# Small constants loaded as rows and spread by one product, the fifth x block in another buffer, and a later last step of the bias table, in a two-layer hybrid trunk

## The chip, the cores and the metric

One core of a Trainium2 chip runs the whole program. The metric is the device time of one execution in microseconds (us), as the median of several runs. Differences are named against the time of the kernel before.

## What is computed

The reference is one inference step of a trunk of two layers, for 512 prompt tokens and 64 sample tokens (576 together) of width 1024, all in fp32. The part that matters here, cut from the reference:

```python
mod = silu(c) @ ada_w + ada_b                 # six pieces: shift, scale, gate, twice
h = rmsnorm(x, norm_mix_g) * (1 + sc_m) + sh_m
z, xbc, dt_raw, q, k, v, g_ssm, g_attn = split(h @ w_in)
dt = softplus(dt_raw + dt_bias);  a = -exp(a_log)      # per SSM head, 32 of them
y = ssd_scan(xs, dt, a, B, C) + xs * d_skip            # per SSM head
q = rmsnorm(q, q_norm_g);  k = rmsnorm(k, k_norm_g)    # 64 values each, per head
p = softmax(concat(q k^T / 8 + bias, sinks))           # sinks: per query head, 16 of them
```

The kernel keeps channels on the 128 partitions. So the constants by heads (`a_log`, `dt_bias`, `d_skip`, `sinks`) are needed repeated on every partition (the last two with even heads on partitions 0 to 63 and odd heads on 64 to 127), and the head norms (`q_norm_g`, `k_norm_g`) are needed as columns, twice one above the other. Then follow the two branches' projections, an output projection, and a gated feed-forward part; all large products go through the same helper.

## The kernel before, in words

**Products.** Each weight block of 1024 x 128 is a granule: SP loads it (L185), ScalarE rounds it to `whi` (L166), GpSimd or VectorE forms the rest `wlo` (L167), and TensorE makes three products for each of 8 blocks of rows and each half of the 576 tokens (L278 to L280): 48 products a projection. ScalarE or VectorE takes the sums out of PSUM.

**The order.** Python code emits instructions in the order of the text; a planner with a simulated timeline then fixes one order for each engine, and for SP's queue of DMAs, and may pull an instruction forward or push it back against the text where its inputs and buffers allow. On the chip each engine goes through its list strictly in order, so an instruction that waits holds all behind it. All DMAs of the kernel are issued on SP.

**The opening.** Five blocks of x (four of 128 tokens, one of 64, in `load_x`, L542) go through a four-buffer ring `w4` and are transposed; the fifth therefore needs a buffer back. The first modulation pieces are loaded in four quarters (L1581) and formed by `ada_quarter`. Three first projections (`leads`, L1615 to L1617) are summed quarter by quarter as the modulated, normalised x (`nt`, `hh`, `hl`) comes. Then a list of jobs runs: in layer 0 the projection for dt (job 0), four q projections, and x, z, B and C ones, with a modulation step (`Ada`, L324) after each from the third job on. Side work (the dt chain, convolution, scan, head norms, attention) is emitted between the pieces of jobs.

**Constants.** `const_loads` loads what lies in DRAM as rows of 128: modulation bias, two norms, scan norm, convolution bias (104 rows, tile `rows`), and convolution weights and state; `const_cols` and `const_rest` transpose them on TensorE (L491, L502, L503). `const_loads1` loads `d_skip`, `dt_bias` and `a_log` already spread over the partitions, `const_loads2` the head norms and the sinks; each tile is first touched by GpSimd (`hold`, L433), so that its load is not issued before some earlier result is there. The Exp of `a_log` stands in `const_rest` (helper line L159, tile `ea`), the negated sinks in `const_nsk` (L486). Layer 0's `const_loads1` is emitted after the last quarter's loads and its `const_loads2` after job 2; layer 1's come at job `C1` = 20 and its readers at job 28.

**The bias table.** `build_bias` is a generator of three steps, taken after the jobs `BI`, `BI+1` and `BI+3` with `BI` = 3: the relative bias is transposed, unrolled into a vector and stored in DRAM (L595); strips of it are loaded back, shifted row by row (L604, tile `rt`); a product with a flipped identity puts them in place (L610, `bflip`), VectorE copies them (L613) and SP stores them (L614). Attention loads the table from there.

Of the kernel before, what the change touches and what calls it, by code (L numbers as in the profile page):

```python
# [12 lines left out]
ALU = mybir.AluOpType  # L13
# [38 lines left out]
def hybrid_trunk(ctx: ExitStack, tc: tile.TileContext, I, O):  # L52
# [376 lines left out]
    after = []  # L429

    def hold(l, t):

        G.tensor_copy(out=t[:, 0:1], in_=L[0]["mod"][:, 2, 0, 0:1] if l else after[0])  # L433

    def const_loads(l):
        c = L[l]
        rowsA = w2("rows", [128, 3, 128])
        rows = c["rows"] = rowsA[:, 2]
        if l:
            hold(l, rows)  # L440
        off = 0
        for src, n in ((I["ada_b"][l], 48), (I["norm_mix_g"][l], 8), (I["norm_ffn_g"][l], 8),
                       (I["ssm_norm_g"][l], 16), (I["conv_b"][l], 24)):
            SY.dma_start(out=rows[off:off + n, :], in_=src.rearrange("(t c) -> t c", c=128))
            off += n
        rowsB = c["rowsB"] = rowsA[:, 0:2]
        if l:
            hold(l, rowsB[:, 0])
            hold(l, rowsB[:, 1])
        SY.dma_start(out=rowsB[0:96, 0, :], in_=I["conv_w"][l].rearrange("k (t c) -> (k t) c", c=128))  # L450
        SY.dma_start(out=rowsB[0:72, 1, :], in_=I["state_conv"][l, 0].rearrange("k (t c) -> (k t) c", c=128))

    def const_loads1(l):
        c = L[l]
        dsk = c["dsk"] = con.tile([128, 16], F32, name=f"dsk{l}")
        hold(l, dsk)
        dv = I["d_skip"][l].rearrange("(m r) -> r m", r=2)
        for r in range(2):
            SY.dma_start(out=dsk[64 * r:64 * r + 64, :], in_=dv[r].partition_broadcast(64))
        dtb = c["dtb"] = con.tile([128, 32], F32, name=f"dtb{l}")  # L460
        hold(l, dtb)
        SY.dma_start(out=dtb, in_=I["dt_bias"][l].partition_broadcast(128))
        ea = c["ea"] = con.tile([128, 32], F32, name=f"ea{l}")
        hold(l, ea)
        SY.dma_start(out=ea, in_=I["a_log"][l].partition_broadcast(128))

    def const_loads2(l):
        c = L[l]
        qkg = con.tile([128, 2], F32, name=f"qkg{l}")
        hold(l, qkg[:, 0:1])  # L470
        hold(l, qkg[:, 1:2])
        for j, nm in enumerate(("q_norm_g", "k_norm_g")):
            for r in range(2):
                SY.dma_start(out=qkg[64 * r:64 * r + 64, j:j + 1], in_=I[nm][l].rearrange("(p o) -> p o", o=1))
        c["qg"], c["kg"] = qkg[:, 0:1], qkg[:, 1:2]
        snk = con.tile([128, 8], F32, name=f"snk{l}")
        hold(l, snk)
        sv = I["sinks"][l].rearrange("(c h) -> h c", h=2)
        for r in range(2):
            SY.dma_start(out=snk[64 * r:64 * r + 64, :], in_=sv[r].partition_broadcast(64))  # L480
        c["snk"] = snk

    def const_nsk(l):
        c = L[l]
        nsk = c["nsk"] = con.tile([128, 8], F32, name=f"nsk{l}")
        V.tensor_scalar(out=nsk, in0=c["snk"], scalar1=-1.0, scalar2=None, op0=ALU.mult)  # L486

    def const_cols(l):
        c = L[l]
        ps = sps("cT")  # L490
        T.transpose(ps[:, 0:104], c["rows"][0:104, :], ident[0:104, 0:104])  # L491
        colA = con.tile([128, 104], F32, name=f"colA{l}")
        V.tensor_copy(out=colA, in_=ps[:, 0:104])
        V.tensor_scalar(out=colA[:, 64:104], in0=colA[:, 64:104], scalar1=0.5, scalar2=None, op0=ALU.mult)
        c["colA"] = colA
        c["ssmg"], c["convb"] = colA[:, 64:80], colA[:, 80:104]
        c["mod"] = con.tile([128, 6, 8, 2], F32, name=f"mod{l}")

    def const_rest(l):
        c = L[l]  # L500
        ps = sps("cB")
        T.transpose(ps[:, 0:96], c["rowsB"][0:96, 0, :], ident[0:96, 0:96])  # L502
        T.transpose(ps[:, 96:168], c["rowsB"][0:72, 1, :], ident[0:72, 0:72])  # L503
        colB = con.tile([128, 4, 24], F32, name=f"colB{l}")
        S.mul(out=colB.rearrange("p k t -> p (k t)"), in_=ps[:, 0:96], mul=0.5)
        stc = con.tile([128, 3, 24], F32, name=f"stc{l}")
        V.tensor_copy(out=stc.rearrange("p k t -> p (k t)"), in_=ps[:, 96:168])
        act(c["ea"], c["ea"], ACTF.Exp)
        c["convw"], c["stc"] = colB, stc
        c["ncv"] = con.tile([128, 2, 3, 24], F32, name=f"ncv{l}")  # L510
# [22 lines left out]
    def load_x(xb):  # L533
# [4 lines left out]
        for i in range(5):  # L538
            n = 128 if i < 4 else 64
            src = I["x_prompt"][0, i * 128:(i + 1) * 128, :] if i < 4 else I["x_sample"][0]  # L540
            xn = w4("xn", [128, 1024])
# [1049 lines left out]
    after.append(raws[3][1][:, 7, 255:256])  # L1591
    const_loads1(0)
# [5 lines left out]
    const_rest(0)  # L1598
    xhs = [next(xgen)]
# [30 lines left out]
    for i, j in enumerate(jobs):  # L1630
# [11 lines left out]
        if i == 2:  # L1642
            after[0] = f32(nm0.hh[1][:, 3, TOK - 1:TOK])
            const_loads2(0)
        if i in (BI, BI + 1, BI + 3):
# [3 lines left out]
        if i == C1:  # L1649
            const_loads(1)  # L1650
            const_loads1(1)
            const_loads2(1)
        if i == C1 + 8:
            const_cols(1)
            const_rest(1)
            for l in range(DEPTH):
                const_nsk(l)
# [39 lines left out]
```

## Time and profile before

| | |
|---|---|
| median of 3 runs | 2643.12 us (2639.3 to 2647.48) |
| the profiled execution | 2642.57 us |
| its span, first to last instruction | 2640.7 us, 49241 instructions |
| mean granted TensorE clock | 0.986 |
| TensorE busy | 2527.7 us (96%), 19605 matmuls |
| VectorE busy | 1605.9 us (61%) |
| ScalarE, GpSimd busy | 1059.0 us, 1054.5 us (40% each) |
| moved by DMA | 294.40 MB, 111 GB/s on average |

Of the span's forty slices of 66 us, the page gives TensorE's busy tenths as 6, 8, 9, 6 for the first four and 9 or more for all others; the granted clock is 8, 9, 9, 7 tenths in those four and 9 in the rest. PE is TensorE, DVE VectorE, ACT ScalarE, POOL GpSimd, and SPq SP's queue of DMAs. An arrow in square brackets gives the idle time before an instruction and what ended it.

### The profile page before, as it was taken

Reading aid. Unit: us, or ns where it says so; the run is one execution under the profiler, and the core shown is the slowest. Engines: PE = TensorE matmul, PEld = TensorE weight load, DVE = VectorE, ACT = ScalarE, POOL = GpSimd, SP = SyncE. Lnnn points to the kernel's source line nnn. Section 1 sums busy time; section 2 is a strip of 40 time slices with the busy share of each in tenths; the row PEclk is TensorE's granted clock in tenths of the full one; section 3 lists DMA queues with packets and bytes.
Section 4 is the critical chain, followed back from the end, with each engine's and each line's share of the span. In section 5 each row is a group of like instructions: output and inputs, shape, how many; then the busy total and the mean of one; then the engine's idle time right before and its main releaser. Section 6 shows DMA issues by size and latency. Waiting matters only on the chain. (4 is left out here: it accounts for less than half of the span.)

```text
span 2640.7 us, 49241 instructions
## 1 busy us (share of the span) xinstructions
PE 2527.7 (96%) x19605; PEld 2399.6 (91%) x19605; DVE 1605.9 (61%) x2981; ACT 1059.0 (40%) x2383; POOL 1054.5 (40%) x980
## 2 busy tenths in 40 slices
PE   6896999999999999999989999999999999999999
PEld 5785898999889999999989899989998899999999
DVE  4376949564765665655576997767456656444443
ACT  3343544433444542222245554544434445323222
POOL 3343544434223774544476544544432257000000
PEclk8997999999999999999999999999999999999999
DMA  7444542333212554544465333232421245322322
GB/s 207 122 154 127 149 114 86 95 83 98 57 49 83 159 166 139 153 152 151 155 175 145 93 111 102 85 95 84 104 72 50 60 128 155 96 87 81 88 77 72
DMA packets 471556, 294.40 MB, mean 111 GB/s; under 512 B 76544, under 2 KB 453856, under 8 KB 471328
## 3 DMA queue, kind: packets, MB, share of 16 engines
q1 hardware_dynamic: 471328, 291.27, 38.4%
q8 instruction: 154, 2.52, 0.4%
q14 instruction: 74, 0.61, 0.1%
HBM read 277.07 MB, written 13.16 MB: 110 GB/s over the span
## 5 line engine op out<-in xcount | busy, mean ns | idle before, releaser
L167 POOL TENSOR_TENSOR wlo<-raw,whi 128x512 fp32r<-128x512 f32 (+1 forms) x632 | 901.4, 1434 | 895.8 <-ACT whi L166 841.2
L278 PE MATMUL dps<-hh,whi 128*128 128x288 f32 x3536 | 1058.8, 300 | 18.6 <-DVE gate L153 13.9
L279 PE MATMUL dps<-hh,wlo 128*128 128x288 f32 x3536 | 1049.6, 297 | 2.8 <-POOL wlo L167 2.8
L280 PE MATMUL dps<-hl,whi 128*128 128x288 f32 x3536 | 1050.2, 297 | 1.1 <-DVE hl L156 1.1
L278 PEld LDWEIGHTS dps<-hh,whi 128*128 128x128 f32 x3536 | 667.0, 189 | 42.8 <-issue 21.5
L166 ACT CAST whi<-raw 128x512 fp32r<-128x512 f32 (+1 forms) x762 | 462.5, 610 | 576.4 <-PE dps L280 424.4
L279 PEld LDWEIGHTS dps<-hh,wlo 128*128 128x128 f32 x3536 | 667.8, 189 | 8.7 <-POOL wlo L167 4.9
L280 PEld LDWEIGHTS dps<-hl,whi 128*128 128x128 f32 x3536 | 667.4, 189 | 6.1 <-issue 4.4
L279 PE MATMUL dps<-ah,wlo 128*128 128x288 f32 x704 | 209.9, 298 | 3.1 <-POOL wlo L167 3.1
L278 PE MATMUL dps<-ah,whi 128*128 128x288 f32 x704 | 207.8, 295 | 4.6 <-DVE x L153 2.4
L280 PE MATMUL dps<-al,whi 128*128 128x288 f32 x704 | 207.7, 295 | 0.0
L153 DVE SCALAR_TENSOR_TENSOR ada_acc<-araw,csl,ada_acc 128x1024 f32<-128x1024 f32 x98 | 149.4, 1563 | 79.7 <-DMA araw<-in_ada_w_dram 73.4
L153 DVE SCALAR_TENSOR_TENSOR cv<-u,colB,cv 128x579 f32<-128x579 f32 x144 | 149.6, 1039 | 38.0 <-ACT cv L159 36.6
L278 PE MATMUL dps<-yh,whi 128*128 128x288 f32 x512 | 153.3, 299 | 9.1 <-ACT u L819 4.3
L280 PE MATMUL dps<-yl,whi 128*128 128x288 f32 x512 | 151.9, 297 | 0.0
L279 PE MATMUL dps<-yh,wlo 128*128 128x288 f32 x512 | 151.3, 296 | 0.0
L278 PEld LDWEIGHTS dps<-ah,whi 128*128 128x128 f32 x704 | 132.1, 188 | 6.1 <-issue 4.2
L279 PEld LDWEIGHTS dps<-ah,wlo 128*128 128x128 f32 x704 | 132.2, 188 | 5.6 <-POOL wlo L167 4.5
L167 DVE TENSOR_TENSOR wlo<-raw,whi 128x512 fp32r<-128x512 f32 (+1 forms) x124 | 83.7, 675 | 87.0 <-ACT whi L166 85.6
L280 PEld LDWEIGHTS dps<-al,whi 128*128 128x128 f32 x704 | 132.2, 188 | 0.2 <-DVE al L167 0.2
L278 PEld LDWEIGHTS dps<-yh,whi 128*128 128x128 f32 x512 | 96.2, 188 | 14.3 <-ACT u L819 5.8
L280 PEld LDWEIGHTS dps<-yl,whi 128*128 128x128 f32 x512 | 96.1, 188 | 1.5 <-issue 1.3
(331 smaller groups left out, 3869.4 us busy)
## 6 DMA issues: line engine op xcount, KB each, us to landing
raw<-in_w_in_dram SPq DMA_DIRECT2D x119, 512.0 KB, 4.0
raw<-in_w_gate_up_dram SPq DMA_DIRECT2D x100, 512.0 KB, 3.9
araw<-in_ada_w_dram SPq DMA_DIRECT2D x56, 512.0 KB, 4.6
bc<-ac_dr SPq DMA_DIRECT2D x32, 512.0 KB, 5.0
raw<-in_w_br_ssm_dram SPq DMA_DIRECT2D x32, 512.0 KB, 3.5
raw<-in_w_out_dram SPq DMA_DIRECT2D x32, 512.0 KB, 4.0
raw<-in_w_down_dram SPq DMA_DIRECT2D x32, 512.0 KB, 4.2
raw<-in_ada_w_dram SPq DMA_DIRECT2D x24, 512.0 KB, 6.3
```

The lines of the kernel that those rows point to most:

```text
L153: V.scalar_tensor_tensor(out=out, in0=in0, scalar=scalar, in1=in1, op0=op0, op1=op1)
L166: S.copy(out=hi, in_=src)
L167: (eng or V).tensor_tensor(out=lo, in0=src, in1=f32(hi), op=ALU.subtract)
L278: T.matmul(ps, lhsT=wh, rhs=rh, start=a == 0, stop=False)
L279: T.matmul(ps, lhsT=wl, rhs=rh, start=False, stop=False)
L280: T.matmul(ps, lhsT=wh, rhs=rl, start=False, stop=a == nk - 1)
```

## The change

The six constants by heads are loaded as three further rows (104, 105, 106) of the tile `rows`: `a_log`, `dt_bias`, `d_skip` and twice `sinks` side by side in row 104, the head norms twice in rows 105 and 106. The transposition takes 107 rows, which gives the head norms as columns. A new function `const_heads` spreads row 104 over all partitions by one product with a repeated unit column; Exp reads `a_log` from its PSUM, and VectorE copies the other three out and negates the sinks. The loads by heads and their holds are gone. The fifth block of x takes a buffer of another ring, `bcs`. The third step of the bias table is taken after job `BI+5` in place of `BI+3`.

```diff
--- before.py
+++ after.py
@@ -426,75 +426,65 @@
 
     L = [dict() for _ in range(DEPTH)]
 
-    after = []
-
-    def hold(l, t):
-
-        G.tensor_copy(out=t[:, 0:1], in_=L[0]["mod"][:, 2, 0, 0:1] if l else after[0])
+    def hold(t):
+
+        G.tensor_copy(out=t[:, 0:1], in_=L[0]["mod"][:, 2, 0, 0:1])
 
     def const_loads(l):
+
         c = L[l]
         rowsA = w2("rows", [128, 3, 128])
         rows = c["rows"] = rowsA[:, 2]
         if l:
-            hold(l, rows)
+            hold(rows)
         off = 0
         for src, n in ((I["ada_b"][l], 48), (I["norm_mix_g"][l], 8), (I["norm_ffn_g"][l], 8),
                        (I["ssm_norm_g"][l], 16), (I["conv_b"][l], 24)):
             SY.dma_start(out=rows[off:off + n, :], in_=src.rearrange("(t c) -> t c", c=128))
             off += n
+        for row, o, nm, rep in ((104, 0, "a_log", 1), (104, 32, "dt_bias", 1), (104, 64, "d_skip", 1),
+                                (104, 96, "sinks", 2), (105, 0, "q_norm_g", 2), (106, 0, "k_norm_g", 2)):
+            src = I[nm][l]
+            n = src.shape[0]
+            SY.dma_start(out=rows[row:row + 1, o:o + rep * n].rearrange("o (r p) -> o r p", r=rep),
+                         in_=bass.AP(tensor=src.tensor, offset=src.offset, ap=[[0, 1], [0, rep], [1, n]]))
         rowsB = c["rowsB"] = rowsA[:, 0:2]
         if l:
-            hold(l, rowsB[:, 0])
-            hold(l, rowsB[:, 1])
+            hold(rowsB[:, 0])
+            hold(rowsB[:, 1])
         SY.dma_start(out=rowsB[0:96, 0, :], in_=I["conv_w"][l].rearrange("k (t c) -> (k t) c", c=128))
         SY.dma_start(out=rowsB[0:72, 1, :], in_=I["state_conv"][l, 0].rearrange("k (t c) -> (k t) c", c=128))
-
-    def const_loads1(l):
-        c = L[l]
-        dsk = c["dsk"] = con.tile([128, 16], F32, name=f"dsk{l}")
-        hold(l, dsk)
-        dv = I["d_skip"][l].rearrange("(m r) -> r m", r=2)
-        for r in range(2):
-            SY.dma_start(out=dsk[64 * r:64 * r + 64, :], in_=dv[r].partition_broadcast(64))
-        dtb = c["dtb"] = con.tile([128, 32], F32, name=f"dtb{l}")
-        hold(l, dtb)
-        SY.dma_start(out=dtb, in_=I["dt_bias"][l].partition_broadcast(128))
-        ea = c["ea"] = con.tile([128, 32], F32, name=f"ea{l}")
-        hold(l, ea)
-        SY.dma_start(out=ea, in_=I["a_log"][l].partition_broadcast(128))
-
-    def const_loads2(l):
-        c = L[l]
-        qkg = con.tile([128, 2], F32, name=f"qkg{l}")
-        hold(l, qkg[:, 0:1])
-        hold(l, qkg[:, 1:2])
-        for j, nm in enumerate(("q_norm_g", "k_norm_g")):
-            for r in range(2):
-                SY.dma_start(out=qkg[64 * r:64 * r + 64, j:j + 1], in_=I[nm][l].rearrange("(p o) -> p o", o=1))
-        c["qg"], c["kg"] = qkg[:, 0:1], qkg[:, 1:2]
-        snk = con.tile([128, 8], F32, name=f"snk{l}")
-        hold(l, snk)
-        sv = I["sinks"][l].rearrange("(c h) -> h c", h=2)
-        for r in range(2):
-            SY.dma_start(out=snk[64 * r:64 * r + 64, :], in_=sv[r].partition_broadcast(64))
-        c["snk"] = snk
-
-    def const_nsk(l):
-        c = L[l]
-        nsk = c["nsk"] = con.tile([128, 8], F32, name=f"nsk{l}")
-        V.tensor_scalar(out=nsk, in0=c["snk"], scalar1=-1.0, scalar2=None, op0=ALU.mult)
 
     def const_cols(l):
         c = L[l]
         ps = sps("cT")
-        T.transpose(ps[:, 0:104], c["rows"][0:104, :], ident[0:104, 0:104])
-        colA = con.tile([128, 104], F32, name=f"colA{l}")
-        V.tensor_copy(out=colA, in_=ps[:, 0:104])
+        T.transpose(ps[:, 0:107], c["rows"][0:107, :], ident[0:107, 0:107])
+        colA = con.tile([128, 107], F32, name=f"colA{l}")
+        V.tensor_copy(out=colA, in_=ps[:, 0:107])
         V.tensor_scalar(out=colA[:, 64:104], in0=colA[:, 64:104], scalar1=0.5, scalar2=None, op0=ALU.mult)
         c["colA"] = colA
         c["ssmg"], c["convb"] = colA[:, 64:80], colA[:, 80:104]
+        c["qg"], c["kg"] = colA[:, 105:106], colA[:, 106:107]
         c["mod"] = con.tile([128, 6, 8, 2], F32, name=f"mod{l}")
+
+    def const_heads(l):
+
+        c = L[l]
+        ps = sps("cH")
+        T.matmul(ps[:, 0:128], lhsT=ident[96:107, 104:105].to_broadcast([11, 128]), rhs=c["rows"][96:107, :],
+                 start=True, stop=True)
+        ea = c["ea"] = con.tile([128, 32], F32, name=f"ea{l}")
+        act(ea, ps[:, 0:32], ACTF.Exp)
+        dtb = c["dtb"] = con.tile([128, 32], F32, name=f"dtb{l}")
+        V.tensor_copy(out=dtb, in_=ps[:, 32:64])
+        dsk = c["dsk"] = con.tile([128, 16], F32, name=f"dsk{l}")
+        snk = c["snk"] = con.tile([128, 8], F32, name=f"snk{l}")
+        for r in range(2):
+            p = slice(64 * r, 64 * r + 64)
+            V.tensor_copy(out=dsk[p], in_=ps[p, 64:96].rearrange("p (m r) -> p r m", r=2)[:, r])
+            V.tensor_copy(out=snk[p], in_=ps[p, 96:112].rearrange("p (m r) -> p r m", r=2)[:, r])
+        nsk = c["nsk"] = con.tile([128, 8], F32, name=f"nsk{l}")
+        V.tensor_scalar(out=nsk, in0=snk, scalar1=-1.0, scalar2=None, op0=ALU.mult)
 
     def const_rest(l):
         c = L[l]
@@ -505,7 +495,6 @@
         S.mul(out=colB.rearrange("p k t -> p (k t)"), in_=ps[:, 0:96], mul=0.5)
         stc = con.tile([128, 3, 24], F32, name=f"stc{l}")
         V.tensor_copy(out=stc.rearrange("p k t -> p (k t)"), in_=ps[:, 96:168])
-        act(c["ea"], c["ea"], ACTF.Exp)
         c["convw"], c["stc"] = colB, stc
         c["ncv"] = con.tile([128, 2, 3, 24], F32, name=f"ncv{l}")
 
@@ -538,7 +527,7 @@
         for i in range(5):
             n = 128 if i < 4 else 64
             src = I["x_prompt"][0, i * 128:(i + 1) * 128, :] if i < 4 else I["x_sample"][0]
-            xn = w4("xn", [128, 1024])
+            xn = (w4 if i < 4 else bcs)("xn", [128, 1024])
             SY.dma_start(out=xn[0:n], in_=src)
             squares = xh[i % 2].rearrange("p k t -> p (k t)")[0:n, 0:1024]
             act(squares, xn[0:n], ACTF.Square, accum_out=ms[0:n, i:i + 1])
@@ -1588,14 +1577,13 @@
                     g.raw = wp.tile([128, 8, 128], F32, tag="raw", bufs=RAWB, name="raw")
                 SY.dma_start(out=g.raw[:, 2 * i:2 * i + 4], in_=g.loads[0][2][:, 2 * i:2 * i + 4])
     gpos["load"] = len(leads)
-    after.append(raws[3][1][:, 7, 255:256])
-    const_loads1(0)
     loads()
     const_cols(0)
     nm0 = L[0]["nrm"] = Norm(0, "mix", xb)
     nm0.alloc()
     ps = [[sps("lead") if g or half else dps() for half in range(2)] for g in range(3)]
     const_rest(0)
+    const_heads(0)
     xhs = [next(xgen)]
     ada_quarter(0, raws[0])
     for i in range(4):
@@ -1639,22 +1627,16 @@
             pump()
         if i == 13:
             spill_x(xb, x_dr[0])
-        if i == 2:
-            after[0] = f32(nm0.hh[1][:, 3, TOK - 1:TOK])
-            const_loads2(0)
-        if i in (BI, BI + 1, BI + 3):
+        if i in (BI, BI + 1, BI + 5):
             if i == BI:
                 bias_gen = build_bias()
             next(bias_gen, None)
         if i == C1:
             const_loads(1)
-            const_loads1(1)
-            const_loads2(1)
         if i == C1 + 8:
             const_cols(1)
             const_rest(1)
-            for l in range(DEPTH):
-                const_nsk(l)
+            const_heads(1)
         if j.post:
             j.post()
     for s in list(sides):
```

## Rows read from the trace of the kernel before

**Rows 1.** Windows: length; busy us (count) PE, PEld, DVE, ACT, POOL; clock; DMA share, GB/s.

```profile
59.00:67.70 8.70, 0.07 (x2) 0.03 (x1) 0.15 (x2) 1.33 (x4) 0.00 (x0) 0.73 0.51 113
67.70:73.10 5.40, 5.40 (x22) 5.23 (x23) 1.64 (x2) 0.69 (x2) 1.83 (x5) 0.50 0.56 124
...
89.60:92.10 2.50, 0.05 (x2) 0.03 (x1) 1.40 (x3) 2.42 (x8) 1.58 (x3) 1.00 0.00 0
...
102.60:105.70 3.10, 0.00 (x0) 0.00 (x0) 2.74 (x6) 0.60 (x3) 1.06 (x2) 1.00 0.26 61
...
120.20:124.30 4.10, 0.07 (x1) 0.00 (x0) 0.00 (x0) 0.56 (x2) 1.76 (x3) 1.00 0.67 164
124.30:127.90 3.60, 3.56 (x9) 2.38 (x10) 1.12 (x2) 0.00 (x0) 0.00 (x0) 0.53 1.05 278
...
194.60:221.70 27.10, 0.01 (x1) 0.03 (x1) 3.38 (x8) 2.90 (x6) 0.00 (x0) 0.59 0.23 67
221.70:227.70 6.00, 5.99 (x36) 4.56 (x36) 6.00 (x8) 2.55 (x5) 3.64 (x4) 0.57 0.48 147
...
300.00:2640.00 2340.00, 2291.21 (x17620) 2191.01 (x17618) 1425.87 (x2668) 941.48 (x2130) 931.89 (x808) 1.00 0.37 107
```

**Rows 2.** Timeline, 22 to 68 us, three engines: start, length, instruction, [idle before].

```profile
22.44 0.22 DVE L507 COPY stc<-cB 128x72 f32<-128x72 f32 x1
...
57.32 0.16 DVE L156 TENSOR_TENSOR mod<-ada_t,colA 128x4 f32<-128x4 f32 x1 [2.65 <-PE ada_t L415]
...
66.37 0.23 ACT L159 ACTIVATE ea<-ea 128x32 f32<-128x32 f32 x1 [14.37 <-DMA ea<-in_a_log_dram]
66.50 0.56 ACT L159 ACTIVATE nt<-xh,mod 128x224 f32<-128x224 f32 x1
...
67.67 0.61 PE L1615 MATMUL dps<-hh,whi 128*128 128x288 f32 x1 [8.63 <-ACT hh L683]
```

**Rows 3.** Timeline, 86 to 106 us, VectorE and TensorE.

```profile
86.10 0.17 DVE L486 TENSOR_SCALAR nsk<-snk 128x8 f32<-128x8 f32 x1 [16.75 <-DMA snk<-in_sinks_dram]
...
92.08 0.41 PE L278 MATMUL dps<-hh,whi 128*128 128x288 f32 x1 [2.45 <-ACT qsq L159]
...
105.70 0.54 PE L782 MATMUL acn<-dtmp,triu 128*128 128x160 f32 x2 [3.14 <-POOL dtmp L778]
```

**Rows 4.** Timeline, 120 to 125 us, SP's queue and TensorE.

```profile
120.00 2.58 SPq L604 DMA_DIRECT2D rt<-vec_dr  x4
...
124.34 2.75 PE L610 MATMUL bflip<-rt,flip 128*128 128x384 f32 x4 [4.08 <-DMA rt<-vec_dr]
```

**Rows 5.** Timeline, 207 to 224 us, layer 1's constants: ScalarE, VectorE, TensorE.

```profile
207.50 0.23 ACT L159 ACTIVATE ea<-ea 128x32 f32<-128x32 f32 x1 [21.42 <-DMA ea<-in_a_log_dram]
...
220.36 0.17 DVE L486 TENSOR_SCALAR nsk<-snk 128x8 f32<-128x8 f32 x1 [9.67 <-DMA snk<-in_sinks_dram]
...
221.71 0.76 PE L873 MATMUL cb<-BC 128*128 128x128 f32 x2 [27.10 <-DVE xT L153]
...
223.31 0.62 ACT L166 CAST whi<-raw 128x512 fp32r<-128x512 f32 x1 [12.91 <-DMA raw<-in_w_in_dram]
```

**Rows 6.** DMA, 184 to 224 us, in forty slices.

```profile
GB/s 0 0 0 0 0 0 0 0 0 0 0 0 0 0 0 0 0 0 0 0 2 134 243 176 4 0 0 0 0 0 0 0 0 119 201 322 381 282 210 74
```

**Rows 7.** Tile of d_skip, whole span: the loads, and issue to landing.

```profile
L459 SPq DMA_DIRECT2D dsk<-in_d_skip_dram x4: 641/672/762, 43.6 to 186.0; - x4
...
DMA to landing us min/median/max: 12.5/16.8/21.1
```

**Rows 8.** Waits of SP's queue, 0 to 20 us: total, times, longest.

```profile
SPq L542 <- DMA xn<-in_x_prompt_dram: 1.3, 1, 1.3
```

**Rows 9.** Tile of the rows, whole span: ns min/median/max, first and last start.

```profile
L444 SPq DMA_DIRECT2D rows<-in_norm_mix_g_dram x2: 315/320/324, 4.0 to 229.3; - x2
...
L491 PE MATMUL cT<-ident,rows x2: 308/344/381, 17.9 to 255.8; 104*128 104x104 f32 x2
...
DMA to landing us min/median/max: 4.2/5.2/6.3
```

## The prediction, made before the change was run

> **What bounds the kernel now.** Start with the profiled execution as a whole: 2642.6 us, of which the span is 2640.7; it stands 0.5 under the median of the three runs, 2643.1, which themselves lie between 2639.3 and 2647.5. So a difference under 0.3% (8 us) can hardly be told from none. TensorE carries the time: from 300 us on it is busy 2291 of 2340 us at a granted clock of 1.00 [rows 1]. No constant is loaded in that stretch, so I expect nothing to be won or lost there. Whatever this change does, it does in the first 230 us.
>
> The windows over the opening show where TensorE stands still there [rows 1]: 59 to 67.7, 89.6 to 92.1, 102.6 to 105.7, 120.2 to 124.3 and, far the longest, 194.6 to 221.7. Behind three of them the clock stands lower while the engine is busy again: 0.50 for 5.4 us, 0.53 for 3.6 us, 0.57 for 6.0 us. A clock of 0.5 is the 1.2 GHz level in place of 2.4. A stop therefore costs its own length and some of the stretch behind it.
>
> Then the timeline says who holds whom. At 57.32 VectorE writes the last quarter of the modulation. ScalarE could use it at once, but its next instruction in order is the Exp of a_log, which waits 14.37 us for its load; the scaling that TensorE needs starts right behind it, at 66.50, and TensorE's 8.63 us end at 67.67 [rows 2]. On VectorE the same is done by the negated sinks: 16.75 us for a load. That is what is late in the next two gaps: a projection waits 2.45 us for the evacuation, and the cumulative sums 3.14 us for the end of the dt chain, which started late on VectorE [rows 3]. The fourth gap is the bias table: the last step's product waits 4.08 us for the strips, whose loads are issued only at 120.00 [rows 4]. The fifth is layer 1's copy of the first: Exp waits 21.42 us, the negated sinks another 9.67, a weight cast 12.91, and TensorE 27.10 at its first score product [rows 5].
>
> Why are these loads slow? With the four-byte pieces of d_skip issued by 186, the queues moved nothing until about 204 (the first twenty of forty one-microsecond slices are zero), and nothing again from 209 to 217, with the sinks' load on the way; d_skip landed 12.5 to 21.1 us after its issue, against 4.2 to 6.3 for constants loaded as rows [rows 6, 7, 9]. One queue serves all of it, so weights issued behind wait as well. The cost lies in many pieces, not in bytes.
>
> **The change, part by part.**
>
> *Loads by heads removed (ten a layer), six rows added.* d_skip had 2 x 64 x 16 = 2048 pieces, the sinks 2 x 64 x 8 = 1024, the head norms 256; the new rows are one or two contiguous runs each. With them go the one-element holds on GpSimd (six a layer), and three loads and their issue time ahead of layer 0's weights on SP.
>
> First gap: the modulation is there at 57.5, scaling and cast take 0.56 and about as much again, and TensorE's own work runs to 59. Nothing remains to wait for: 8.6 us, and half of the 5.4 us at 0.50, 2.7 [rows 1, 2]. Gain 11.3; between 8.6, if the clock still falls for another reason, and 11.3.
>
> Second and third gap: VectorE loses its 16.75 us wait and starts the convolution and the dt chain as soon as data comes. TensorE too comes 11.3 us earlier, so VectorE keeps 16.75 - 11.3, some 5 us, of lead over what it ends today. Together 2.5 + 3.1 = 5.6; bounds 0 and 5.6; I take 5.0, near the upper end, as both waits are shorter than that lead [rows 1, 3].
>
> Layer 1: Exp no longer stands in ScalarE's queue, the negated sinks no longer in VectorE's. Behind the removed Exp come a convolution, the decay and a cast, all with their inputs there. So the 27.1 us go, and of the 6.0 at 0.57 another 2.6: 29.7 [rows 1, 5]. Against it stand layer 1's new operations. Take 28.7; bounds 25.8 and 29.7, the lower being 27.1 less 1.3 for copies and no clock regained.
>
> *Spreading product and its readers.* One matmul of 11 rows by 128 columns, nearest the row transposition, 0.38 us; the Exp stays one of 0.23; dt_bias, two halves each of d_skip and sinks, and the negation are six VectorE instructions, at most as long as the 0.22 us copy of 72 columns from PSUM [rows 2, 9]: 1.3 us a layer. In layer 1 TensorE has work of its own meanwhile; if VectorE is the bound there, they cost their 1.3, which is the lower bound above. The negation is only moved. The transposition of 107 rows in place of 104 costs nothing I could see.
>
> *Opening, SP queue.* The fifth x block went out late: its issue waited 1.3 us on an earlier x load [rows 8], besides its buffer. In its own buffer that can be gained. The six new loads cost 0.32 each to issue [rows 9], 1.9, ahead of the other weights, modulation quarters among them. Net 0.6 lost; call it 0.7. Bounds: a gain of 1.3, if the issues hide behind transfers in flight, and a loss of 1.9 + 1.3 = 3.2 with the six copies on the path of the first norm as well. Nothing reads layer 0's rows before the x blocks are transposed, so their landing is covered by that; without that cover the wait falls on TensorE (the rival below).
>
> *Loading many small things: a rule against this.* The rows show constants issued 0.32 us apart that land within 6.3 us of their issue [rows 9]; the term above takes 0.32 each. The Trainium skill ("DMA: Bandwidth & Descriptors", Rules for kernel authors) says the opposite of a list of small transfers: coalesce them, under 64 KB one mostly pays overhead, with about 2 us fixed for one. By that the six would be an estimated 12 us in series and the gain of the whole some 39 us. I go by the row.
>
> *Bias table's last step two jobs later.* It takes four flip products, four copies on VectorE and four stores on SP past one projection and one modulation step. A projection has 48 products, and the late stretch makes one in 2291 / 17620 = 0.13 us [rows 1]: its strips have then 6.2 us more where 4.08 were missing. So the 4.1 us go and of the 3.6 at 0.53 another 1.7: 5.8 [rows 1, 4]. Take 5.0; bounds 0 (the planner pulls the step forward again) and 5.8. The stores on SP now stand beside other weight loads, and the table is first read by layer 0's attention, many projections later, so nobody waits for them.
>
> **Sum.** 11.3 + 5.0 + 28.7 - 0.7 + 5.0 = 49.3. Profiled 2642.6 - 49.3 = 2593.3; with the 0.5 to the median 2593.8. All upper ends, 11.3 + 5.6 + 29.7 + 1.3 + 5.8 = 53.7, give 2589.4; all lower ends, 8.6 + 0 + 25.8 - 3.2 + 0 = 31.2, give 2611.9.
>
> **Rivals.**
>
> *The small gaps stay.* TensorE comes to the second, third and fourth gap 11 us earlier and meets VectorE, GpSimd and the strips earlier too. For it: the strips' chain is a round trip through memory that no longer has an earlier start; against it: VectorE's wait of 16.75 goes in full. Gain 11.3 + 28.7 - 0.7 = 39.3: 2603.8.
>
> *The weights were late anyway.* The 12.91 us wait of the cast in layer 1 [rows 5] stays and TensorE with it. Against it: for most of that time no bytes moved [rows 6]. Gain 49.3 - 12.9 = 36.4: 2606.7.
>
> *Small loads in series.* Each of the six waits on SP like the x load, 1.3, plus 0.32: 9.7 in place of 1.9 in the opening, so 7.8 more: 2601.6. The Trainium skill's rule above is this one.
>
> *Slower: the wait moves to TensorE.* The planner puts the transposition of the rows soon behind their loads, as it put the Exp behind a_log's; TensorE then stands until the last of 13 loads is there. Were they as slow as d_skip, 21.1, with 13 x 0.32 = 4.2 of issue and 2.7 of lower clock, that is 28.0 a layer, 56.0 in both, against 49.3 gained: 6.7 slower, 2649.8. It decides from a landing of 17.8 us on. For it speaks how Exp was placed, against it 4.2 to 6.3 for rows of this very kind [rows 9]; about 18 us would leave the time as it was.
>
> *The change not doing what it says:* the planner may leave the fifth x block where it was; that lies within the opening's bounds.
>
> **Numbers.** Forecast 0.72; small gaps stay 0.09; late weights 0.07; loads in series 0.06; wait on TensorE 0.06, half of it near no change, half slower. All but the last are faster by far more than 0.3%: faster 0.94, same 0.03, slower 0.03. The point is the forecast's, rounded, 2594. The range takes in all its bounds and the three faster rivals, 2589 to 2612, with 3 more below for the spread of the runs: 2586 to 2612.
>
> **What would show it.** Right: no Exp or negation waiting on a load; TensorE without a gap from about 40 us on, and at clock 1.00 there; layer 1's first score product with no wait, some 50 us earlier; the queues moving weights all the while; the flip product without a wait. The order on SP of x, rows and modulation shows the opening's term. Wrong: a transposition of rows that waits on a load; a cast in layer 1 still waiting over 10 us for weights; VectorE or GpSimd ending TensorE's waits before 130 us; a stretch beyond 300 us whose length has changed by more than a few us.

## The result, and the profile after

| | before | after |
|---|---|---|
| median, beside each other on one chip | 2641.56 us (2639.3 to 2647.48, 4 runs) | 2599.44 us (2596.11 to 2600.57, 4 runs) |
| ratio, 95% interval | | 0.9838 [0.9826, 0.9851] |
| profiled execution, its span | 2642.57, 2640.7 us | 2600.57, 2598.9 us |
| mean granted clock | 0.986 | 0.992 |

The change gains 42 us, 1.6%, where 49.3 were forecast; the time lies within the range given. In the spans the gain is 2640.7 - 2598.9 = 41.8, and this section follows these 41.8 through the span.

First the parts of the page on busy time and on the forty slices:

```profile
PE 2530.2 (97%) x19609; PEld 2399.9 (92%) x19609; DVE 1601.8 (62%) x2991; ACT 1061.5 (41%) x2383; POOL 1043.4 (40%) x968
...
PE   7999999999999999999999999999999999999999
```

TensorE is busy as long as before, 2530 us, so what went is idle time. After the first slice it is busy for nine tenths or more everywhere; before, the first four were 6, 8, 9 and 6, and one further on was 8.

The windows of after (columns as in [rows 1]):

```profile
61.70:67.70 6.00, 5.94 (x43) 5.71 (x44) 1.52 (x3) 2.03 (x7) 1.60 (x2) 1.00 0.46 92
67.70:103.70 36.00, 35.56 (x277) 32.12 (x276) 20.78 (x36) 18.07 (x52) 20.26 (x50) 1.00 0.37 104
...
150.00:230.00 80.00, 80.00 (x682) 70.23 (x681) 73.87 (x136) 42.33 (x84) 42.36 (x40) 1.00 0.51 153
```

From 67.7 to 103.7 us TensorE is idle for 0.44, and from 150 to 230, where layer 1's constants are loaded and read, not at all. Its clock is 1.00 in both, and in the row above them too, behind the last quarter's first product, where it was 0.50 for 5.4 us [rows 1]. The second and third gap of [rows 1] belong to the stretch up to 103.7, the fifth to the one from 150.

The timeline of after, TensorE from 29 to 181 us. These are the instructions that answer to [rows 2, 3, 4, 5], and every wait over 1 us behind the first product:

```profile
29.64 0.61 PE L1603 MATMUL dps<-hh,whi 128*128 128x288 f32 x1 [7.76 <-ACT hh L672]
...
61.73 0.41 PE L1603 MATMUL dps<-hh,whi 128*128 128x288 f32 x1 [0.43 <-ACT hh L672]
...
71.48 0.63 PE L738 MATMUL dtn<-stack,dtT 64*128 64x32 f32 x4
...
91.48 0.43 PE L771 MATMUL acn<-dtmp,triu 128*128 128x160 f32 x2
...
104.97 0.67 PE L1082 MATMUL qs<-qsq,sel 128*32 128x288 f32 x2 [1.23 <-ACT qsq L159]
...
111.12 1.45 PE L599 MATMUL bflip<-rt,flip 128*128 128x384 f32 x4
...
135.46 0.30 PE L860 MATMUL xn<-ident,xT 128*64 128x128 f32 x1 [1.92 <-DVE xT L153]
...
141.74 0.30 PE L860 MATMUL xn<-ident,xT 128*64 128x128 f32 x1 [0.88 <-DVE xT L153]
...
180.44 0.49 PE L862 MATMUL cb<-BC 128*128 128x128 f32 x2
```

The last quarter's product waits 0.43 us instead of 8.63, the cumulative sums, the flip product and layer 1's first score product for nothing, instead of 3.14, 4.08 and 27.10. Three waits are new: 1.23 at the query scaling, 1.92 and 0.88 at the transposed x, 4.0 together.

To see what each stretch gave, take the same product in both timelines and subtract its starts, before less after:

| product | before | after | ahead by |
|---|---|---|---|
| first of the first quarter (L1615, now L1603) | 28.62 | 29.64 | -1.0 |
| first of the last quarter | 67.67 | 61.73 | 5.9 |
| first transposition of dt (dtn) | 79.69 | 71.48 | 8.2 |
| first cumulative sum (acn) | 105.70 | 91.48 | 14.2 |
| 25th modulation product of the jobs (ada_ps) | 130.47 | 112.50 | 18.0 |
| 17th transposition of x (xn) | 189.47 | 175.37 | 14.1 |
| 25th transposition of x | 259.71 | 217.11 | 42.6 |
| end of the span | 2640.7 | 2598.9 | 41.8 |

First gap and opening gave 8.2 (the 2.3 from 5.9 to 8.2 lie where the clock no longer falls), second and third 6.0, the bias table's stretch 3.8 and then took back 3.9, layer 1 gave 28.5, the rest lost 0.8. A second profile of the same kernel (`e11_bias_far_alone`, below) gives 5.2, 6.0, 3.5, -4.0, 26.5 and 1.9: the parts in the middle repeat within 0.3 us, the opening's, layer 1's and the rest only within 2 to 3.

Two things in after were not in the forecast. First, the opening. SP's queue, 3 to 27 us:

```profile
3.45 0.58 SPq L531 DMA_DIRECT2D xn<-in_x_sample_dram  x1
...
7.98 4.12 SPq L1570 DMA_DIRECT2D ada<-in_ada_w_dram  x4
12.14 0.36 SPq L449 DMA_DIRECT2D rows<-in_a_log_dram  x1
...
14.95 0.56 SPq L449 DMA_DIRECT2D rows<-in_k_norm_g_dram  x1
17.33 0.34 SPq L455 DMA_DIRECT2D rows<-in_conv_w_dram  x1
18.77 0.31 SPq L456 DMA_DIRECT2D rows<-in_state_conv_dram  x1
19.12 2.81 SPq L1578 DMA_DIRECT2D raw<-in_w_in_dram  x3
21.98 5.38 SPq L1570 DMA_DIRECT2D ada<-in_ada_w_dram  x6
```

The planner put eight small loads between the first modulation quarter and the first weights; in before one stood there, at 11.69, and the other convolution load had gone out at 6.50, ahead of the quarter. From the first of them to the weights pass 7.0 us, and the weights are issued at 19.12; in the timeline of before that is 12.46. The timeline of ScalarE, VectorE and GpSimd, 20 to 29 us (GpSimd from 21):

```profile
23.33 0.62 ACT L166 CAST whi<-raw 128x512 fp32r<-128x512 f32 x1 [2.90 <-DMA raw<-in_w_in_dram]
23.85 0.19 ACT L159 ACTIVATE ea<-cH 128x32 f32<-128x32 f32 x1
...
28.91 0.67 ACT L672 CAST hh<-nt 128x576 fp32r<-128x576 f32 x1 [2.08 <-DVE nt L665]
...
24.07 0.19 DVE L479 COPY dtb<-cH 128x32 f32<-128x32 f32 x1 [2.84 <-ACT ea L159]
...
24.86 1.12 DVE L153 SCALAR_TENSOR_TENSOR mod<-mod,colA 128x4 f32<-128x4 f32 x1
...
26.08 1.12 DVE L487 TENSOR_SCALAR nsk<-snk 128x8 f32<-128x8 f32 x1
...
20.78 5.18 POOL L558 TENSOR_TENSOR xh<-x,bcw 128x1152 f32<-128x1152 f32 x2
25.92 1.26 POOL L167 TENSOR_TENSOR wlo<-raw,whi 128x512 fp32r<-128x512 f32 x1
```

A cast waits for the late weights, the Exp stands behind the cast, VectorE's copies are put down as waiting for the Exp, and the modulation stands behind the copies. (GpSimd's two lines are taken up in the last section.)

Second, the weights of layer 0's projections. ScalarE, 100 to 135 us, casts of a weight, three of after and then one of before:

```profile
103.62 0.62 ACT L166 CAST whi<-raw 128x512 fp32r<-128x512 f32 x1 [5.45 <-DMA raw<-in_w_in_dram]
...
114.69 0.62 ACT L166 CAST whi<-raw 128x512 fp32r<-128x512 f32 x1 [6.71 <-DMA raw<-in_w_in_dram]
...
132.75 0.62 ACT L166 CAST whi<-raw 128x512 fp32r<-128x512 f32 x1 [4.61 <-DMA raw<-in_w_in_dram]
...
129.26 0.62 ACT L166 CAST whi<-raw 128x512 fp32r<-128x512 f32 x1 [8.50 <-DMA raw<-in_w_in_dram]
```

The casts waited for weights here before as well, and both TensorE and the issue of the loads come some 14 us earlier now. What differs is where the waits fall: in before one cast waits 8.50 us beside TensorE's stop at the flip product, and those behind it, up to 150 us, for no load; in after, without that stop, casts wait 6.71, 3.04 and 4.61 us one after the other. The activation behind the last of these casts releases the transposed x, for which TensorE waits at 135.46.

### The profile page after: what moved, and what is told of

Same layout as the page of the kernel before. It is cut to its first block, busy times and chain, and to the rows that moved or that the text cites. A ratio compares the mean times of both kernels' runs of the same rounds, so it can differ in the third digit from the quotient of the medians.

```text
span 2598.9 us, 49232 instructions
## 1 busy us (share of the span) xinstructions
PE 2530.2 (97%) x19609; PEld 2399.9 (92%) x19609; DVE 1601.8 (62%) x2991; ACT 1061.5 (41%) x2383; POOL 1043.4 (40%) x968
```

## The experiments

All times are beside runs of the kernel before on the same chip. "Before" and "after" name the kernel an edit starts from.

**The three parts alone.** Each of the first three kernels has one part of the change.

```diff
--- before.py
+++ e1_x_only
-            xn = w4("xn", [128, 1024])
+            xn = (w4 if i < 4 else bcs)("xn", [128, 1024])
--- before.py
+++ e2_bias_only
-        if i in (BI, BI + 1, BI + 3):
+        if i in (BI, BI + 1, BI + 5):
--- after.py
+++ e3_constants_only
-            xn = (w4 if i < 4 else bcs)("xn", [128, 1024])
+            xn = w4("xn", [128, 1024])
-        if i in (BI, BI + 1, BI + 5):
+        if i in (BI, BI + 1, BI + 3):
```

> The kernel before with the fifth x block in the other ring and nothing else. Theory: the opening's small term. The x block's load no longer waits; the planner now issues it ahead of the rows, and convolution weights and states go behind the first modulation quarter; time within 3 us of before, all later gaps of TensorE as before (8.6, 2.5, 3.1, 4.1, 27.1). Rival (the x block bought part of the 42 us): more than 5 us faster.

> The kernel before with the bias table's last step after job BI+5 and nothing else. Theory of the prediction: the flip product waits no more, 4 to 6 us faster, up to 5 of it kept. Rival (the time is given back behind it, as the stretch from 130 to 160 us of the changed kernel suggests, where ScalarE waits for weights and TensorE for the transposed x): the gap at 120 goes, and a later gap of 1 to 3 us appears; 1 to 3 us faster.

> The changed kernel with the fifth x block back in its old ring and the bias step back after BI+3: the constants alone. Theory: nearly all of the gain is here, 36 to 41 us faster than before, with gaps 1, 2, 3 and 5 gone and the flip product waiting about 4 us again. Rival (the three parts need each other): under 33 us.

Measured: the fifth x block alone 2640.04 us, ratio 0.9996 [0.9986, 1.0005]; the bias step alone 2640.86, 0.9994 [0.9984, 1.0004]; the constants alone 2600.71, 0.9842 [0.9827, 0.9856]. So the whole gain is in the constants, and the other two parts are worth nothing that a run can show. TensorE's timeline with the bias step alone tells why:

```profile
120.97 0.67 PE L1093 MATMUL qs<-qsq,sel 128*32 128x288 f32 x2 [1.76 <-ACT qsq L159]
...
155.68 0.30 PE L871 MATMUL xn<-ident,xT 128*64 128x128 f32 x1 [0.88 <-DVE xT L153]
```

The flip product waits no longer, and two other instructions wait in its place.

**Readers or queue, in layer 1.** Two reasons could explain the 27 us: the loads in many pieces hold the queue, and what stands behind them comes late; or the readers (Exp, negated sinks) hold their engines. The kernel after, with layer 1's `d_skip` and `sinks` loaded by heads as before into tiles that nothing reads, tells them apart; its companion does so with `dt_bias` and `a_log`, 128 pieces of 128 bytes each.

```diff
--- after.py
+++ e4_dead_loads
             const_loads(1)
+            for nm, per in (("d_skip", 16), ("sinks", 8)):
+                t = con.tile([128, per], F32, name=f"dead_{nm}")
+                hold(t)
+                dv = I[nm][1].rearrange("(m r) -> r m", r=2)
+                for r in range(2):
+                    SY.dma_start(out=t[64 * r:64 * r + 64, :], in_=dv[r].partition_broadcast(64))
--- after.py
+++ e5_dead_rows
             const_loads(1)
+            for nm in ("dt_bias", "a_log"):
+                t = con.tile([128, 32], F32, name=f"dead_{nm}")
+                hold(t)
+                SY.dma_start(out=t, in_=I[nm][1].partition_broadcast(128))
```

> The changed kernel plus layer 1's d_skip and sinks loaded by heads, as in the kernel before, into tiles that nobody reads (four loads of 1024, 1024, 512 and 512 four-byte pieces, issued with layer 1's constants). Theory one (many pieces hold the queue, and weights behind them wait): no bytes move for some 18 and 9 us, a cast of weights waits over 10 us, TensorE stands for 5 to 20 us though nothing reads these tiles. Theory two (only the readers in order, Exp and the negation, made TensorE wait): under 2 us slower than the changed kernel, no new gap.

> The changed kernel plus layer 1's dt_bias and a_log loaded on every partition (two loads of 128 contiguous pieces of 128 bytes, 16 KB each) into tiles that nobody reads. Theory one in its form 'the number of pieces sets the price': 256 pieces in place of 3072, under 2 us slower than the changed kernel, queues not idle for more than 3 us. Rival (any load spread over partitions is slow): over 5 us slower.

Measured: 2629.35 us, ratio 0.9947 [0.993, 0.9964], and 2602.69 us, 0.985 [0.9836, 0.9865]. The unread loads by heads give back 29.9 of the 42 us; the 256 larger pieces 3.3, near what a run can tell (after itself had 2601.81 when it was measured again, below). The timeline of the first, four engines:

```profile
171.61 1.36 SPq L1641 DMA_DIRECT2D dead_d_skip<-in_d_skip_dram  x2
173.07 7.91 SPq L1641 DMA_DIRECT2D dead_sinks<-in_sinks_dram  x2
181.03 7.52 SPq L185 DMA_DIRECT2D raw<-in_ada_w_dram  x1
...
207.38 0.62 ACT L166 CAST whi<-raw 128x512 fp32r<-128x512 f32 x1 [29.35 <-DMA raw<-in_w_in_dram]
...
209.90 2.05 DVE L156 TENSOR_TENSOR seg<-bc,ac 128x1024 f32<-128x1024 f32 x1 [27.11 <-DMA bc<-ac_dr]
...
212.60 1.76 PE L921 MATMUL yp<-bc,S 128*64 128x128 f32 x14 [26.49 <-DVE S L156]
```

Its DMA view from 172 to 212 us, in one-microsecond slices:

```profile
GB/s 0 0 0 0 0 0 0 0 0 0 0 0 0 0 0 0 0 0 0 0 0 0 0 0 17 0 0 0 9 152 179 305 372 382 364 367 261 171 62 33
```

Nothing is read, and the queue stands still for about 28 us all the same, to 200: a weight cast waits 29.35 us, the decay 27.11 for its own round trip, and TensorE 26.49, as it waited 27.10 before [rows 5]. The gap in layer 1 is the queue's; its readers were not needed for it. TensorE waits here for the decay, whose round trip stands in the queue behind the pieces as the weights do; in before it went on right behind the negation, so there the readers stood in the chain as well. In these two runs the number of pieces sets the price, not the bytes: 3072 pieces of four bytes (12 KB) take the 28.4 us from 171.6 to 200, 9.2 ns a piece, and 256 pieces with 32 KB cost next to nothing. The Trainium skill ("DMA: Bandwidth & Descriptors", Measured) gives about 10.5 ns a packet for a load of 4 KB on another path, issued from GpSimd; the run agrees in size.

**The same question in layer 0.** The kernel after with layer 0's `d_skip` by heads, unread, behind the modulation quarters and ahead of the query weights, as before had it.

```diff
--- after.py
+++ e10_one_dead_load
+    t = con.tile([128, 16], F32, name="dead0")
+    G.tensor_copy(out=t[:, 0:1], in_=raws[3][1][:, 7, 255:256])
+    dv = I["d_skip"][0].rearrange("(m r) -> r m", r=2)
+    for r in range(2):
+        SY.dma_start(out=t[64 * r:64 * r + 64, :], in_=dv[r].partition_broadcast(64))
```

> The kernel after, plus layer 0's d_skip loaded by heads (2048 pieces of four bytes) at the place where the kernel before issued it, into a tile that nothing reads. Theory one, the first gap came from the readers standing in order (Exp on ScalarE behind a_log's load): no reader, no gap at the last quarter's scaling; TensorE waits there under 1 us, any later wait for weights is under 3 us, time 2598 to 2603. Theory two, as in layer 1 the queue itself is what stops: the queues move nothing for 2048 x 9.2 ns = 18.8 us behind the quarters, the query weights behind it land that much later, and TensorE waits 5 to 12 us for a weight cast at its first products behind the quarters; time 2605 to 2615.

Measured: 2602.38 us, ratio 0.9854 [0.9837, 0.987]. Its DMA view from 44 to 84 us, in one-microsecond slices:

```profile
GB/s 286 236 140 101 192 7 0 0 0 0 0 0 0 0 0 0 0 0 0 0 0 0 0 38 157 214 223 328 269 264 182 311 168 192 269 51 0 0 0 0
```

The timeline of the same kernel, TensorE:

```profile
62.12 0.40 PE L1608 MATMUL dps<-hh,whi 128*128 128x288 f32 x1 [0.43 <-ACT hh L672]
...
73.37 0.63 PE L738 MATMUL dtn<-stack,dtT 64*128 64x32 f32 x4 [1.41 <-ACT dtT L730]
```

The queue is silent for 17 us, from 50 to 67, and TensorE waits 0.43 us at the last quarter and 1.41 behind it. So in layer 0 the answer is the other one: without a reader in order the gap does not come back. TensorE works on for 9.8 us from 62.12, and what had stopped it in before was the Exp in front of the scaling. (Of the loads that before had there, this run has `d_skip` alone; `dt_bias` and `a_log`, 256 larger pieces, are left out.) A silent queue costs 0.6 to 2.9 us in layer 0, by the two medians of after, hardly to be told from nothing, and some 27 in layer 1.

**Is the bias step worth anything behind the new constants?** After, with only that step back at its old place.

```diff
--- after.py
+++ e6_bias_back
-        if i in (BI, BI + 1, BI + 5):
+        if i in (BI, BI + 1, BI + 3):
```

> The changed kernel with the bias step back after BI+3. Forecast's term: 5 us slower than the changed kernel. What its trace suggests (the gain is given back from 130 us on): 0 to 3 us slower, with a wait of 2 to 4 us at the flip product and less of a wait at the transposed x behind it.

Measured: 2599.43 us, ratio 0.9841 [0.9826, 0.9856]; after has 2599.44. TensorE's timeline:

```profile
110.79 2.90 PE L599 MATMUL bflip<-rt,flip 128*128 128x384 f32 x4 [4.16 <-DMA rt<-vec_dr]
```

The flip product waits 4.16 us again, and the waits at the query scaling and the transposed x are gone. TensorE waits about 4 us in this stretch at either place. Not in every execution: in the profiles of `e5_dead_rows` and `e10_one_dead_load`, which have the step where after has it and TensorE in the same order, the waits at the transposed x are missing, and 1.32 and 0.61 us at the query scaling are all. So what comes back lies between 0.6 and 4 us, and the medians show no gain.

**What the opening costs.** Two steps: first the readers of layer 0's row 104 are emitted behind the quarters, then the six loads too, with the head norms' columns by a second small product.

```diff
--- after.py
+++ e7_heads_late
     const_rest(0)
-    const_heads(0)
...
         g.raw = None
+    const_heads(0)
--- e7_heads_late
+++ e8_loads_late
...
+        if l:
+            head_loads(l)
...
+        T.matmul(ps[:, 128:139], lhsT=c["rows"][96:107, :], rhs=ident[96:107, 96:107], start=True, stop=True)
+        qkg = con.tile([128, 2], F32, name=f"qkg{l}")
+        V.tensor_copy(out=qkg, in_=ps[:, 137:139])
...
+    head_loads(0)
```

> The changed kernel with layer 0's const_heads emitted after the four quarters, the loads left where they are. Theory (in the opening the spreading product's readers stand before the modulation on VectorE, and Exp stands behind a weight cast that waits for late weights): the first rounded x comes 2 us earlier than the changed kernel's 28.9 us, time 1 to 3 us faster than the changed kernel. Rival (the loads' order alone costs it): no change within 1 us.

> As e7, and layer 0's six new loads issued behind the last modulation quarter, their columns formed by a second small product in const_heads. Theory: the first projections' weights and modulation quarters are issued 3 to 5 us earlier; first rounded x at 26.5 to 27 us, and 2 to 5 us faster than the changed kernel in all: about 2595. Rival (TensorE is bound by the sums in the quarters anyway): as e7.

Measured: 2597.86 us, ratio 0.983 [0.9813, 0.9846], and 2595.7 us, 0.9826 [0.9812, 0.9841]. ScalarE's cast for the first product starts at 29.13 with the readers late, against 28.91 in after: the readers' place alone brings nothing. With the loads late, ScalarE and SP in the opening:

```profile
12.88 3.80 SPq L1586 DMA_DIRECT2D raw<-in_w_in_dram  x3
...
26.01 0.67 ACT L680 CAST hh<-nt 128x576 fp32r<-128x576 f32 x1 [2.35 <-DVE nt L673]
```

The weights are issued 6.2 us earlier and the cast comes 2.9 earlier; TensorE's first transposition of dt starts at 67.65 instead of 71.48. In eight profiles with the six loads in front it starts at 70.45 to 74.45, in three with the loads late (this one and two below) at 66.79 to 67.65. So the place of the small loads on SP is what the opening lost. The medians fall by 1.6 and another 2.2, which is within the spread of the runs (2592.56 to 2600.98 for the second).

**A better version?** The bias table out of the crowded stretch altogether, its three steps 41 jobs later, on top of the late loads; this kernel is measured twice.

```diff
--- e8_loads_late
+++ e9_bias_far, e12_best_again
-    BI = 3
+    BI = 44
```

The kernel that ran as `e11_bias_far_alone` is not the one that its expectation describes. Its `BI` is 3: it is the kernel after, line for line. So it measures after a second time, beside `e12_best_again` on one chip, and the table moved alone was never run.

> The kernel after, with layer 0's small loads behind the quarters (as e8_loads_late) and the bias table's last step 44 jobs later, behind layer 1's last score step. Theory, the bias table's own loads, stores and strips crowd the stretch from 95 to 145 us: the waits of e8_loads_late at 101.8 (1.81, query scaling) and at 131.7 and 138.0 (1.40 and 0.89, transposed x) go, and the time is 2 to 5 us under e8_loads_late's 2595.7: 2591 to 2594. Rival, the stretch is crowded by the weights themselves and their casts: such waits stay, by 2 us or more together, and the time is 2594 to 2598.

> The kernel after with all three steps of the bias table's build 41 jobs later and nothing else changed, so the late small loads are left out of it. Theory, e9_bias_far's step over e8_loads_late (3.5 us) is the bias table's own: the waits of after at 135.46 and 141.74 (1.92 and 0.88, transposed x) go and the time is 2.5 to 4 us under after's 2599.4, at 2595 to 2597. Rival, it came with the late loads or with the spread of runs: 2598 to 2601.

> e9_bias_far once more, beside e11_bias_far_alone on one chip. Theory, both moves add up: 2591 to 2594 again, and 2 to 4 us under e11_bias_far_alone, which is what layer 0's small loads cost in the opening. Rival, the late loads are worth nothing that lasts: both kernels within 1.5 us.

Measured: with late loads and the table far away 2592.16 us, ratio 0.9819 [0.9804, 0.9833], and again 2592.06 us, 0.9805 [0.9792, 0.9819]; after, again, 2601.81 us, 0.9847 [0.9834, 0.986]. TensorE's timeline of `e11_bias_far_alone` shows the flip products at their place in after, and the waits of after:

```profile
108.15 0.67 PE L1082 MATMUL qs<-qsq,sel 128*32 128x288 f32 x2 [1.45 <-ACT qsq L159]
...
114.33 1.45 PE L599 MATMUL bflip<-rt,flip 128*128 128x384 f32 x4
...
138.37 0.30 PE L860 MATMUL xn<-ident,xT 128*64 128x128 f32 x1 [1.59 <-DVE xT L153]
```

ScalarE's casts of a weight, two with the late loads alone (`e8_loads_late`) and two with the table far away as well (`e9_bias_far`):

```profile
111.25 0.62 ACT L166 CAST whi<-raw 128x512 fp32r<-128x512 f32 x1 [6.42 <-DMA raw<-in_w_in_dram]
...
128.97 0.62 ACT L166 CAST whi<-raw 128x512 fp32r<-128x512 f32 x1 [4.15 <-DMA raw<-in_w_in_dram]
...
112.29 0.62 ACT L166 CAST whi<-raw 128x512 fp32r<-128x512 f32 x1 [1.24 <-PE dps L280]
...
127.76 0.62 ACT L166 CAST whi<-raw 128x512 fp32r<-128x512 f32 x1 [1.13 <-PE dps L280]
```

With both moves no cast between 101 and 145 us waits for a load, in either profile; TensorE's waits at the transposed x are gone, and that at the query scaling stays (1.25 and 2.32). So the theory that the bias table's own traffic crowds this stretch fits the casts and the transposed x and not the query scaling; but the planner put other work in another order around the moved steps too, which no run separates. The two moves together are worth 9.75 us beside after on one chip, with intervals apart, and 7 by after's first median. Of these the loads alone bring some 4 by the medians, and the table's move another 3.5, where the intervals overlap (0.9826 [0.9812, 0.9841] with the late loads alone). What the table's move brings without the late loads is open.

## Why the prediction was right, and where it was off

**The first gap (11.3, less 0.7 for the opening): measured 8.2.** The mechanism is shown: with the queue as silent as before and no reader, there is no gap. The term that failed is the opening's. It took 0.32 us for the issue of each new load, a bare issue time, and a loss of 0.7 in all. The six started 0.3 to 1.1 us apart, and behind them, still in front of the first weights, came the two convolution loads; by the waits of SP's queue these two stood 1.8 and 1.1 us for the quarter. (With the fifth x block moved alone they stood there too, and waited for nothing.) Against 10.6 for gap and opening together 2.4 are missing; with the 0.7 that makes a loss of 3.1, at the bound named, 3.2; by the second profile of after it is 6.1, beyond it. With the loads late the two together give 12.0 to 12.9, so the gap's 11.3 is there. The rival of loads in series had this mechanism, but priced it at 7.8 more; the six went out within 2.8 us. The gain put on the fifth x block was not there: its load went out at 3.45 us instead of 8.20 also in the kernel with that part alone, and the time was the same.

**The second and third gap (5.0): measured 6.0.** Both are gone. The lead that VectorE was to have sufficed. With the bias table back at its old place they are gone too, so it is the constants' doing.

**Layer 1 (28.7): measured 28.5.** The size is right and the reason is half wrong. The working took the gap from the readers, Exp first, then the negation, then a late cast. The run with unread loads shows that the queue alone makes a gap as long. The sentence that one queue serves all and that weights behind the pieces wait names the cause, and it stood there as a side remark. That is also why the rival of weights late anyway fell: they were late through the same pieces, and came with them. By its working, loads that nobody reads should have left most of layer 1's gain; they left almost none.

**The bias step (5.0): measured nothing.** This step of the prediction failed. It reckoned the strips' wait of 4.08 and a lower clock behind it as gone, and did not ask which wait ends next. The casts wait for weights in this stretch, up to 6.71 us; with TensorE's stop at the flip product the casts behind it had their weights. Without it TensorE runs on into the query scaling and the transposed x, and gives back 3.9, all of the 3.8 it had won (in other executions less, see above). It is what the rival of the small gaps that stay described, at one of its three places. That late weights bound this stretch is read from the casts, and that the table's own traffic makes them late from the runs with the table far away, which had the late loads as well; a deeper ring of weight buffers was not tried.

**The spreading product and its readers (1.0 of layer 1's term).** Cheap, as taken: the product takes 0.27 to 0.37 us, Exp 0.19, the copies 0.15 to 0.19. Only the negation took longer, 1.12 in the opening and 1.18 in layer 1; the last section takes this up.

**Beyond 230 us (0): measured -0.8** in the profiled pair. It is no step of the change that a run here could show: the second profile of after has +1.9 there, and eight executions of after lie between 2596.11 us at a mean clock of 0.997 and 2603.8 at 0.992.

Together: 49.3 - 2.4 + 1.0 - 0.2 - 5.1 - 0.8 = 41.8, that of the spans.

## What to carry to other kernels

Count the pieces of a load, not its bytes: a constant spread by DMA element by element held up every load behind it on the queue here, for some 9 ns a piece, so load it as a row and spread it with one small product. When an engine waits behind such a load, ask separately who holds the engine and who holds the queue, by a load that nobody reads; and before pricing a removed wait in full, look for the next late input in that stretch. The new small loads cost the place they took in the queue, not their issue time: put such loads behind the first weights.

## What was not expected of the hardware

Four-byte pieces came at 8 to 9 ns each whatever was queued behind them: 2048 pieces in 17 us in layer 0, 3072 in 28 us in layer 1. Loads issued afterwards, to other tiles, moved nothing until they were through. The Trainium skill ("DMA: Bandwidth & Descriptors", Two DMAs through the same engine are not ordered) says that within one queue of one DMA engine descriptors start in order; the runs agree with that, though all loads here use one queue and none shows what a second one would do.

The negation of eight columns took 1.12 us in the opening, where the same form took 0.17 before [rows 3]. It ended at 27.20, and GpSimd's weight remainder, which began at 25.92, at 27.18. The modulation ahead of it, 24.86 to 25.98, ended likewise with GpSimd's scaling of x, at 25.96. The Trainium skill ("SBUF — State Buffer", Who interferes with whom) says that VectorE and GpSimd share a pair of ports, that a VectorE instruction needs these beside its own when it has two inputs in SBUF or runs in a mode with two ports, and that whichever of the two engines comes first keeps them for its whole instruction while the other is blocked. The trace agrees for these two. Other rows bear it out: VectorE's negation in the opening of `e10_one_dead_load`, and in layer 1 of `e8_loads_late`.

```profile
25.62 2.47 DVE L487 TENSOR_SCALAR nsk<-snk 128x8 f32<-128x8 f32 x1
...
218.24 0.16 DVE L495 TENSOR_SCALAR nsk<-snk 128x8 f32<-128x8 f32 x1
```

The first stands beside GpSimd's scaling of x, from 25.45 to 28.05, and ends 0.03 us behind it; the second has no GpSimd instruction beside it.
